# Entry to a paged decode stage: the order of the first key transposes, the third weight's cast, a zero fill and a third store buffer

## The chip, the cores and the metric

The kernel runs on one core of a Trainium2 chip. The metric is the device time of one execution in microseconds (us), lower is better. A core has TensorE (PE in the profile, with its weight loads as PEld), VectorE (DVE), ScalarE (ACT), GpSimd (POOL) and SyncE (SP). SP, ACT and POOL also issue DMA transfers, all of which run on the same 16 DMA engines of the core. Each engine works through its own instructions in their order; an instruction that waits for another engine or for a transfer holds up all that stands behind it on its engine.

## What is computed

The reference is one layer of a hybrid decoder for 512 prompt tokens and 32 sample tokens (8 sequences of 4), model width 1024:

```
h = x + 0.5 * post1(SwiGLU_1(pre1(x)))
u = pre_mix(h); z = u @ w_in
    4 HGRN2 heads: gated linear recurrence
    4 MLA heads: softmax attention on 256 latent + 64 rotary columns
h = h + post_mix(concat(o_hgrn, o_mla) @ w_out)
y = h + 0.5 * post2(SwiGLU_2(pre2(h)))
```

The sample tokens attend to 4096 past positions, which lie in a paged pool in HBM and are gathered through a page table. All is float32. The kernel forms a float32 product of two matrices as three products of float32r parts: each operand is split into a high part (a cast) and a low part (the operand less its high part), and high x high, high x low and low x high are added up in PSUM.

## The kernel before

Activations lie transposed, 128 features on the partitions and tokens along the free dimension. A weight is loaded in blocks of 128 output columns: `weight` (L211 to L220) issues a 512 KB load on SP's queue into one of five buffers `wraw`, casts it on ACT to the high part (L218) and subtracts on DVE for the low part (L219). The parts go to one of two buffer pairs `wh`, `wl`, or to a buffer that the caller passes as `home`. A raw buffer is free again after the subtract, and only then can SP load the next weight into it.

The stages follow each other: the first SwiGLU block (up to 390 us in the profile), the input projection with the recurrent heads (to 600), prompt attention (to 700), a long stage in which the decode attention of the sample tokens runs beside the output projection of the second prompt half and the first third of the second SwiGLU block (700 to 980), and the rest of the second SwiGLU block.

The change lies in the entry to that long stage, and in one buffer near its end. Two generators share the engines there. `phase_a` (L719) is the dense side. It starts with `project(1, ...)` (L664): the output projection of prompt half 1 in eight columns `d` of 128 features. Columns 0 and 1 are one `gemm_2` (L248), which does seven of the eight inner blocks of both and leaves the last, which needs the last attention head, to the end. Columns 2 to 7 are a `gemm_q` each (L237): 24 matmuls of 256 tokens. The weight `wo(d)` of columns 2 and 5 goes to a home of its own, a tile with the tag `hl`, so that it does not wait for `wh` and `wl`; the others rotate through the two pairs. In before, the cast and the subtract of `wo(2)` are written behind the two columns of `gemm_2` and their copies out of PSUM (`column`, L682). Beside this runs `squares(0)` (L706), which stores the finished half 0 and sums its squares (L711, L713). After the projection come SwiGLU columns of 512 prompt tokens (`gate`, `up`), and after every four of them `downs` (L751): eight partial products `d`, each copied out of PSUM by ACT (L755) into a tile `sit`, of which there are two, and stored to HBM from ACT's queue (L756). `downs` runs twice; the second pass (c = 1) lies at 944 to 978 us. Beside its last columns runs `sample_u` (L1345), whose sum of squares (L1364 on ACT, then the product at L1331 on PE) stands in the same queues.

`decode` (L1532) is the other side. For each half sequence (`Half`) it gathers two blocks of latent rows of 1 MB each (`gather`, L1455, POOL's queue) and two blocks of rotary rows of 256 KB (`gather_r`, L1464), then transposes them in five turns on DVE (`turn`, L1471, ten transposes of 32x32 blocks called `kh`), multiplies them with the queries (`score`, L1479), and so on. The first turn of a half takes the rotary blocks `rraw`, the other four the latent blocks (`ma` and `dx` for the first half). The weights of the softmax are spread into a tile `pbuf` (L1443), whose other places must be zero: POOL fills it (L1444), in before as the first thing in the stage, ahead of the gathers.

The two generators are advanced in turns by a fixed rule (L1616 to L1627); a scheduling pass then sets each engine's order. `tc.issue_after(i)` puts the instructions of its block behind instruction `i` in the order of their engine. `turn` uses it already for a half's last turn.

Of the kernel before, what the change touches and what calls it, by code (L numbers as in the profile page):

```python
# [8 lines left out]
F32 = mybir.dt.float32  # L9
# [5 lines left out]
ALU = mybir.AluOpType  # L15
# [92 lines left out]
def hybrid_step_kernel(  # L108
# [18 lines left out]
    def mk(shape, dt, tag, bufs=1, pool=None):  # L127
        return (pool or cur[-1]).tile(shape, dt, name=tag, tag=tag, bufs=bufs)
# [16 lines left out]
    def f32(ap):  # L145
        return ap.bitcast(F32)
# [61 lines left out]
    def rstd_u(u, x):  # L208
        return rstd(u[2], sumsq([h[x][:, k] for k in range(KD)]), D)

    def weight(srcs, kt, staged=False, home=None):  # L211
        pool, sfx, bufs = (st, "x", STAG) if staged else (sb, "", NW)
        w = mk([P, 8, P], F32, "wraw", 5, pool=sb)
        wh, wl = home or [mk([P, 8, P], F32R, n + sfx, bufs, pool=pool) for n in ("wh", "wl")]
        n = P // len(srcs)
        for i, s in enumerate(srcs):
            nc.sync.dma_start(w[:, :kt, i * n : (i + 1) * n], s)
        nc.scalar.copy(wh[:, :kt], w[:, :kt])  # L218
        nc.vector.tensor_tensor(wl[:, :kt], w[:, :kt], f32(wh[:, :kt]), op=ALU.subtract)  # L219
        return wh, wl, kt  # L220

    def mm3(out, pairs):
# [38 lines left out]
    def wcols(w, k0, kt, c0):  # L261
        return w[c0 // P, :, k0 : k0 + kt]
# [401 lines left out]
    def project(x, o, nxt, pool=None):  # L664
        if x:
            h[x] = actslot("m", 1, n=HS[0])
        else:
            qts.append(mk([P, 2 * KQ * HS[0]], F32, "q0", pool=dK))
            h[x] = qts[0][:, : KD * HS[0]].rearrange("p (k t) -> p k t", k=KD)
        nc.sync.dma_start(h[x], hsp[:, :, prompt[x]])  # L670
        yield
        mT = mk([P, KD, HS[0]], F32, "hh", pool=pool) if pool else actslot("m", x, n=HS[0])
        sacc = tmp("ssq", HS[0])

        def wo(d):
            home = None
            if pool and d % 3 == 2:
                home = mk([P, 2, KD, P], F32R, "hl", pool=pool)
                home = home[:, 0], home[:, 1]
            return weight([wcols(w_o, 0, KD, d * P)], KD, home=home)  # L680

        def column(d, acc):  # L682
            nc.scalar.copy(mT[:, d], acc)
            scale_sq(sacc, mT, d, gv, 3)

        d0 = 0
        if pool:
            for d, acc in enumerate((yield from gemm_2([wo(d) for d in range(2)], o))):
                column(d, acc)
            d0 = 2  # L690
            yield
        for d in range(d0, KD):
            column(d, (yield from gemm_q(wo(d), o, 4)) if pool else gemm(wo(d), o))
            yield
        yield from post(x, mT, sacc, None, nxt)

# [22 lines left out]
    def phase_a():  # L719
        acc = None  # L720
        full = slice(0, TP)

        def pair():
            return [mk([P, CA, TP], F32R, n, pool=ffa) for n in ("hh", "hl")]

        def col(w, f, cs=full, step=2):
            return gemm_q(w, [t[:, :, cs] for t in u4[:2]], step)

        def wt(w, f):
            return weight([wcols(w[1], 0, KD, f * P)], KD)  # L730

        def swish(s, z, cs):
            t = mk([P, TP], F32, "sit", 2, pool=ffa)[:, cs]
            nc.vector.tensor_tensor(s, z, u4[2][:, cs], op=ALU.mult)
            sigmoid(t, s)
            nc.vector.tensor_tensor(s, s, t, op=ALU.mult)

        def gate(f):
            s = mk([P, TP], F32, "sil", 1, pool=ffa)
            z = yield from col(wt(w_g, f), f)  # L740
            yield
            swish(s, z, full)
            return s

        def up(f, s):
            z = yield from col(wt(w_u, f), f)
            yield
            nc.vector.tensor_tensor(s, s, z, op=ALU.mult)
            split(hh[:, f % CA], hl[:, f % CA], s)

        def downs(c):  # L751
            for d in range(KD):
                acc = yield from gemm_q(weight([wcols(w_d[1], c * CA, CA, d * P)], CA), (hh, hl), 2)
                t = mk([P, TP], F32, "sit", 2, pool=ffa)
                nc.scalar.copy(t, acc)  # L755
                nc.scalar.dma_start(mA[c][:, d], t)  # L756
                yield

        pj = project(1, oo[1], to_ffn, ffa)
        next(pj)  # L760
        sq = squares(0)
        for n, _ in enumerate(pj):
            acc = next(sq, None) or acc
            if n == 9:
                root(0, acc)
            yield
            if n == 14:
                break
        s = mk([P, TP], F32, "sil", 1, pool=ffa)
        w, v = wt(w_g, 0), wt(w_u, 0)  # L770
        ups = []
        for x in BOTH:
            z = yield from col(w, 0, prompt[x], 4)
            yield
            ups.append((yield from col(v, 0, prompt[x], 4)))
            if x:
                root(1, acc)
            yield
            swish(s[:, prompt[x]], z, prompt[x])
            if x == 0:  # L780
                nc.vector.tensor_tensor(s[:, prompt[0]], s[:, prompt[0]], ups[0], op=ALU.mult)
                for _ in pj:
                    pass
                *_, acc = squares(1)
        hh, hl = pair()
        nc.vector.tensor_tensor(s[:, prompt[1]], s[:, prompt[1]], ups[1], op=ALU.mult)
        split(hh[:, 0], hl[:, 0], s)
        for c in range(FA // CA):
            for f in range(c * CA, (c + 1) * CA):
                if f:  # L790
                    s = ahead if f and f % CA == 0 else (yield from gate(f))
                    if f and f % CA == 0:
                        hh, hl = pair()
                    yield from up(f, s)
            if c + 1 < FA // CA:
                ahead = yield from gate(f + 1)
            yield from downs(c)
# [599 lines left out]
    with scope("dec"):  # L1397
# [43 lines left out]

        slots = ("ma", "dx0", "dx1", "q0", "ha", "hb", "mb")
        pbuf = mk([P, 2, 2, ROWS, 32], F32, "pbuf")  # L1443
        nc.gpsimd.memset(pbuf, 0.0)  # L1444
        NH2 = 2 * NB

        class Half:
# [84 lines left out]
        def decode():  # L1532
# [9 lines left out]
            def turn(top):  # L1542
                if ups:
                    h_, st = ups.pop(0)
                    with tc.issue_after(top.ins) if top is not None else nullcontext():
                        h_.turn(st)
                    if st == 0 and h_.n + 1 < NH2:
                        H[h_.n + 1].gather_r()

            for n in range(NH2 + 4):  # L1550
# [4 lines left out]
                for st in range(len(JS)):  # L1555
# [3 lines left out]
                    if n < 2 and st == 0:  # L1559
                        if n == 0:  # L1560
                            H[0].gather_r()
                        gather(2)
                    if n == 2 and st == 3:
                        gather(3)
                    if st == PEAK and at(3):
# [353 lines left out]
```

## Time and profile before

| what | value |
|---|---|
| time, median of 3 runs | 1246.13 us |
| the three runs | 1246.13, 1246.31, 1241.62 us |
| the profiled execution's own time | 1246.37 us |
| its span in the trace | 1244.6 us |
| PE busy | 1210.0 us, 97% of the span |
| DVE / ACT / POOL busy | 981.5 / 702.8 / 93.1 us |
| moved by DMA | 190.70 MB, 153 GB/s in the mean |

The profiled execution is 0.24 us above the median. Its time is 1.77 us longer than the span of its trace, which begins with the first and ends with the last instruction. In an answer of the trace, a row of the timeline gives the start, the duration, the engine, the line, the operation with its output and inputs, their shapes and how many such instructions were merged; in brackets stands the idle time of the engine just before, and what ended it. Matmuls overlap, so the distance of their starts, not their duration, is the pace. A row of the windows gives, for a stretch, each engine's busy time with the instructions in brackets, the granted TensorE clock (1.00 is full speed), the share of the DMA engines' time that was in use and the rate.

### The profile page before, as it was taken

How to read it: one execution, taken by the hardware profiler on the slowest of the kernel's cores; microseconds unless marked ns; L12 is line 12 of the kernel's file. 1: busy time of each engine (PE TensorE's matmuls, PEld its weight loads, DVE VectorE, ACT ScalarE, POOL GpSimd, SP SyncE). 2: the span in 40 equal slices, each digit the busy share in tenths (PEclk: the TensorE clock that was granted, in tenths of full speed). 3: DMA queues.
4: the chain of work that ended last, by engine and by line, in shares of the span. 5: the costliest groups of instructions: out<-in, count | busy, mean ns of one | idle time of the engine just before them, and what ended most of it. 6: DMA issues, size and time to landing. Idle time of an engine off the chain costs nothing.

```text
span 1244.6 us, 29432 instructions
## 1 busy us (share of the span) xinstructions
PE 1210.0 (97%) x12216; PEld 1114.2 (90%) x12216; DVE 981.5 (79%) x1994; ACT 702.8 (56%) x1524; POOL 93.1 (7%) x106
## 2 busy tenths in 40 slices
PE   8999999999999999999999799999999999999997
PEld 7999999999999989988998687776777899999996
DVE  7897788878678888786877779998885679778765
ACT  7675545444466745445758566555554446555373
POOL 0000000000000000000000212332320011000100
PEclk9999999999999999999999799999999999999998
DMA  6232333233164213333242676679775666833561
GB/s 238 86 119 87 101 103 102 86 102 98 52 228 141 79 59 100 100 82 102 93 137 82 216 276 204 227 277 358 267 258 169 242 242 231 226 120 103 117 146 73
DMA packets 80518, 190.70 MB, mean 153 GB/s; under 512 B 14064, under 2 KB 37648, under 8 KB 75904
## 3 DMA queue, kind: packets, MB, share of 16 engines
q1 hardware_dynamic: 58128, 115.50, 28.4%
q0 software_dynamic: 16368, 65.67, 16.2%
q10 hardware_dynamic: 5888, 7.65, 1.8%
q8 instruction: 96, 1.57, 0.5%
q14 instruction: 38, 0.31, 0.1%
HBM read 172.63 MB, written 16.16 MB: 152 GB/s over the span
## 4 chain that ended last, share of the span: by engine, by line
PE 80%; DVE 7%; issue 6%; DMA 4%; ACT 3%; POOL 0%; DVEq 0%; SPq 0%; POOLq 0%
PE acc L245 19%; PE dn L227 12%; PE Y L446 9%; PE acc L227 9%; PE Z L446 6%; PE X L446 6%; PE acc L1821 3%; PE acc L624 3%; PE s L1488 3%; PE o L1521 2%; DMA ma<-w_g 1%; DVE kh L1476 1%; PE pa L962 1%; PE s L1215 1%; DMA wraw<-w_u 1%
## 5 line engine op out<-in xcount | busy, mean ns | idle before, releaser
L245 PE MATMUL acc<-uh,wh 128*128 128x272 f32 (+2 forms) x496 | 161.7, 326 | 0.5 <-ACT uh L195 0.5
L245 PE MATMUL acc<-ul,wh 128*128 128x272 f32 (+2 forms) x496 | 156.6, 316 | 0.9 <-DVE ul L196 0.9
L245 PE MATMUL acc<-uh,wl 128*128 128x272 f32 (+2 forms) x496 | 155.7, 314 | 0.0
L219 DVE TENSOR_TENSOR wl<-wraw,wh 128x1024 fp32r<-128x1024 f32 (+2 forms) x78 | 83.8, 1075 | 37.0 <-ACT wh L218 36.7
L218 ACT CAST wh<-wraw 128x1024 fp32r<-128x1024 f32 (+2 forms) x78 | 72.6, 933 | 69.9 <-PE acc L245 62.4
L227 PE MATMUL dn<-hh,dh 128*128 128x272 f32 x384 | 111.6, 291 | 0.2 <-DVE hb L495 0.2
L227 PE MATMUL dn<-hh,dl 128*128 128x272 f32 x384 | 110.6, 288 | 0.0
L227 PE MATMUL dn<-hl,dh 128*128 128x272 f32 x384 | 110.5, 288 | 0.0
L245 PEld LDWEIGHTS acc<-uh,wh 128*128 128x128 f32 x496 | 93.3, 188 | 15.1 <-issue 9.9
L245 PEld LDWEIGHTS acc<-ul,wh 128*128 128x128 f32 x496 | 93.4, 188 | 7.1 <-issue 1.6
L245 PEld LDWEIGHTS acc<-uh,wl 128*128 128x128 f32 x496 | 93.3, 188 | 6.1 <-issue 1.1
L227 PEld LDWEIGHTS dn<-hh,dh 128*128 128x128 f32 x384 | 72.3, 188 | 1.4 <-DVE hb L495 0.4
L227 PEld LDWEIGHTS dn<-hl,dh 128*128 128x128 f32 x384 | 72.5, 189 | 0.0
L227 PEld LDWEIGHTS dn<-hh,dl 128*128 128x128 f32 x384 | 72.1, 188 | 0.0
L158 ACT CAST wh<-wraw 128x512 fp32r<-128x512 f32 (+1 forms) x67 | 41.0, 651 | 40.3 <-PE Z L446 22.6
L158 ACT CAST sh<-wraw 128x512 fp32r<-128x512 f32 (+1 forms) x66 | 40.6, 657 | 38.4 <-PE Z L446 26.0
L158 ACT CAST dh<-wraw 128x512 fp32r<-128x512 f32 x48 | 29.8, 621 | 45.5 <-PE dn L227 44.2
L159 DVE TENSOR_TENSOR wl<-wraw,wh 128x512 fp32r<-128x512 f32 (+1 forms) x67 | 47.1, 727 | 7.9 <-ACT wh L158 7.4
L1488 PE MATMUL s<-kh,q 64*32 64x128 f32 x2560 | 49.5, 273 | 2.3 <-issue 2.3
L1512 ACT COPY pbuf<-pt 32x64 f32<-32x64 f32 x192 | 46.5, 242 | 8.0 <-DVE pt L1508 5.2
L1488 PEld LDWEIGHTS s<-kh,q 64*32 64x32 f32 x2560 | 37.8, 105 | 13.7 <-issue 9.8
L159 DVE TENSOR_TENSOR sl<-wraw,sh 128x512 fp32r<-128x512 f32 (+1 forms) x66 | 46.7, 736 | 1.9 <-ACT sh L158 0.8
(720 smaller groups left out, 4117.2 us busy)
## 6 DMA issues: line engine op xcount, KB each, us to landing
wraw<-w_u SPq DMA_DIRECT2D x44, 512.0 KB, 4.0
wraw<-w_g SPq DMA_DIRECT2D x43, 512.0 KB, 3.7
wraw<-w_d SPq DMA_DIRECT2D x24, 512.0 KB, 3.9
wraw<-w_in SPq DMA_DIRECT2D x24, 512.0 KB, 3.6
wraw<-w_o SPq DMA_DIRECT2D x16, 512.0 KB, 3.6
wraw<-w_d SPq DMA_DIRECT2D x16, 384.0 KB, 3.1
wraw<-w_d SPq DMA_DIRECT2D x16, 256.0 KB, 4.1
mA<-sit ACTq DMA_DIRECT2D x16, 256.0 KB, 5.5
```

The costliest lines, as they stand in the source:

```text
L158: nc.scalar.copy(hi, src)
L159: (eng or nc.vector).tensor_tensor(lo, src, f32(hi), op=ALU.subtract)
L218: nc.scalar.copy(wh[:, :kt], w[:, :kt])
L219: nc.vector.tensor_tensor(wl[:, :kt], w[:, :kt], f32(wh[:, :kt]), op=ALU.subtract)
L227: nc.tensor.matmul(out, a, b, start=n == 0, stop=n == last)
L245: nc.tensor.matmul(acc[:, :n], a[:, k], b[:, k], start=k + i == 0, stop=k == kt - 1 and i == 2)
L446: nc.tensor.matmul(bank, a[p][:, k], b[q][:, k], start=first and k + n == 0, stop=k == 3 and n == 2, skip_group_check=True)
L624: nc.tensor.matmul(accs[x, d], wts[d][p][:, k], hs[k // 2][q][:, k % 2, x], start=k + n == 0, stop=k == nf - 1 and n == 2)
L1488: nc.tensor.matmul(self.s[r][c * 32 : c * 32 + 32, :P], q[rs, j], kh, start=st + jj == 0, stop=st == len(JS) - 1 and jj == 1, skip_group_c ...
L1512: (nc.scalar.copy if g else nc.vector.tensor_copy)(self.p[g * 32 : g * 32 + 32, c // 2, c % 2 * 4 : c % 2 * 4 + 4, self.i * 16 : self.i * ...
L1521: nc.tensor.matmul(o[g : g + 32, :R], self.p[:, c, a], self.craw[c][:, a], start=i + c == 0 and a < 4, stop=i + c == 2 and a >= 4, skip_gr ...
L1821: nc.tensor.matmul(accs[x, d], wts[d][p][:, k], hs[k // 2][q][:, k % 2, x], start=k + n == 0, stop=k == nf - 1 and n == 2)
```

## The change

Four edits:

1. `project` makes the weights of columns 0, 1 and 2 before the first product when it runs in `phase_a`. The cast and subtract of `wo(2)` so stand ahead of the copies of columns 0 and 1.
2. `weight` notes its subtract in `low`, `project` keeps that of `wo(3)` in `pin`, and the first turn of the first half goes through `issue_after` behind it.
3. The zero fill of `pbuf` is issued behind the first three gathers of latent rows.
4. In the second pass of `downs`, columns 2 and 5 use the tile `sil`, by then idle, as a third store buffer.

```diff
+    low = [None]
+    pin = [None]
...
-        nc.vector.tensor_tensor(wl[:, :kt], w[:, :kt], f32(wh[:, :kt]), op=ALU.subtract)
+        low[0] = nc.vector.tensor_tensor(wl[:, :kt], w[:, :kt], f32(wh[:, :kt]), op=ALU.subtract)
...
-            return weight([wcols(w_o, 0, KD, d * P)], KD, home=home)
+            w = weight([wcols(w_o, 0, KD, d * P)], KD, home=home)
+            if d == 3:
+                pin[0] = low[0]
+            return w
...
         if pool:
-            for d, acc in enumerate((yield from gemm_2([wo(d) for d in range(2)], o))):
+            w = [wo(d) for d in range(3)]
+            for d, acc in enumerate((yield from gemm_2(w[:2], o))):
                 column(d, acc)
             d0 = 2
             yield
         for d in range(d0, KD):
-            column(d, (yield from gemm_q(wo(d), o, 4)) if pool else gemm(wo(d), o))
+            wt = w[2] if pool and d == 2 else wo(d)
+            column(d, (yield from gemm_q(wt, o, 4)) if pool else gemm(wt, o))
...
-                t = mk([P, TP], F32, "sit", 2, pool=ffa)
+                n = c and d % 3 == 2
+                t = mk([P, TP], F32, "sil" if n else "sit", 1 if n else 2, pool=ffa)
...
         pbuf = mk([P, 2, 2, ROWS, 32], F32, "pbuf")
-        nc.gpsimd.memset(pbuf, 0.0)
...
                 if ups:
                     h_, st = ups.pop(0)
+                    if h_.n + st == 0:
+                        top = pin[0]
                     with tc.issue_after(top.ins) if top is not None else nullcontext():
                         h_.turn(st)
...
                         gather(2)
+                        if n:
+                            nc.gpsimd.memset(pbuf, 0.0)
```

Line numbers of the new kernel are up to twelve higher. On DVE at the entry to the stage, from the last step of half 0's activations (`ul`) on, this stood in before (`q_8242` is half 0 of the activations, `hl` is the weight of column 2, then of column 5, `wl` those of the columns between, `kh<-rraw` the two halves of the first key turn, `ssq` sums of squares):

```order
L196 SCALAR_TENSOR_TENSOR ul<-q_8242,gv,uh 128x256 x4
L268 TENSOR_TENSOR ssq<-ssq,sq_8856 128x256
L1476 STREAM_TRANSPOSE kh<-rraw 128x512
L713 TENSOR_TENSOR ssq<-ssq,sq_8860 128x256
L1476 STREAM_TRANSPOSE kh<-rraw 128x512
L219 TENSOR_TENSOR hl<-wraw,hl 128x1024
L713 TENSOR_TENSOR ssq<-ssq,sq_8881 128x256
L219 TENSOR_TENSOR wl<-wraw,wh 128x1024 x2
L1476 STREAM_TRANSPOSE kh<-ma 128x512 x3
```

And this stands there now:

```order
L196 SCALAR_TENSOR_TENSOR ul<-q_8242,gv,uh 128x256 x4
L222 TENSOR_TENSOR hl<-wraw,hl 128x1024
L271 TENSOR_TENSOR ssq<-ssq,sq_8860 128x256
L721 TENSOR_TENSOR ssq<-ssq,sq_8864 128x256
L721 TENSOR_TENSOR ssq<-ssq,sq_8880 128x256
L222 TENSOR_TENSOR wl<-wraw,wh 128x1024 x2
L222 TENSOR_TENSOR hl<-wraw,hl 128x1024
L271 TENSOR_TENSOR ssq<-ssq,sq_8896 128x256
L721 TENSOR_TENSOR ssq<-ssq,sq_8900 128x256
L1484 STREAM_TRANSPOSE kh<-rraw 128x512
L721 TENSOR_TENSOR ssq<-ssq,sq_8922 128x256
L1484 STREAM_TRANSPOSE kh<-rraw 128x512
```

The subtract for column 2 has moved to the front, and both transposes of the first key turn now stand behind the subtracts for columns 3, 4 and 5; those of the latent blocks follow between the subtracts for columns 6 and 7. On ACT, the last three columns of the second `downs` pass, from the cast of column 5's weight on, stood so in before (`mA` is the HBM buffer of the stores; the rows of L1355, L185, L186 and L1364 are those of `sample_u`):

```order
L218 CAST wh<-wraw 128x512
L755 COPY sit<-acc 128x512
L1355 ACTIVATE s_post<-tp 128x256
L756 DMA mA_4783<-sit 128x512
L158 CAST wh<-wraw 128x1024
L755 COPY sit<-acc 128x512
L185 ACTIVATE rs_t<-tS,epst 128x32
L756 DMA mA_4783<-sit 128x512
L186 ACTIVATE sS<-rs_t 128x32
L158 CAST wh<-wraw 128x1024
L755 COPY sit<-acc 128x512
L1364 ACTIVATE s_post<-ssq 128x256
```

And so now:

```order
L221 CAST wh<-wraw 128x512
L764 COPY sil<-acc 128x512
L1364 ACTIVATE s_post<-tp 128x256
L765 DMA mA_4783<-sil 128x512
L158 CAST wh<-wraw 128x1024
L764 COPY sit<-acc 128x512
L185 ACTIVATE rs_t<-tS,epst 128x32
L765 DMA mA_4783<-sit 128x512
L186 ACTIVATE sS<-rs_t 128x32
L158 CAST wh<-wraw 128x1024
L764 COPY sit<-acc 128x512
L1373 ACTIVATE s_post<-ssq 128x256
```

The order is the same, but column 5's copy has a buffer of its own, so that the copy of column 7 takes over the buffer of column 4's store and no longer that of column 5's.

## The prediction

> **What bounds the kernel now.** I read the page first, its slices of the span:
>
> ```profile
> PE   8999999999999999999999799999999999999997
> ```
>
> PE is over 90% busy in every slice except the first, the last and one in the middle, the 23rd (684 to 715 us). So PE paces the kernel, and time is to be had only where it waits. The view of the waits, for PE over the whole span, says where; its columns are total, number and longest:
>
> ```profile
> PE acc L245 <- DVE hl L219: 4.1, 1, 4.1
> PE acc L245 <- ACT hl L218: 3.3, 1, 3.3
> PE pr L1331 <- ACT s_post L1364: 2.6, 1, 2.6
> ```
>
> The first two are one place: column 2 of the projection waits for the high and then the low part of its weight `hl`. The third lies some 270 us later. Next I read the stretches around both places; behind the busy times stand clock, DMA share and GB/s:
>
> ```profile
> 702.00:704.00 2.00, 0.00 (x0) 0.00 (x0) 0.88 (x3) 2.00 (x7) 1.40 (x3) 0.59 1.00 334
> 701.66:709.80 8.14, 0.80 (x3) 0.50 (x2) 4.02 (x9) 5.44 (x12) 6.02 (x7) 0.54 0.97 317
> 709.80:715.95 6.15, 6.14 (x29) 6.15 (x30) 5.55 (x8) 1.05 (x2) 0.78 (x1) 0.50 1.01 420
> 715.95:730.20 14.25, 14.25 (x117) 14.09 (x117) 8.94 (x15) 11.03 (x25) 1.18 (x1) 1.00 0.81 302
> 978.13:982.20 4.07, 4.07 (x19) 4.02 (x20) 3.01 (x5) 1.34 (x4) 0.00 (x0) 0.59 0.43 165
> 982.20:984.45 2.25, 2.25 (x19) 2.21 (x18) 2.25 (x3) 0.00 (x0) 0.00 (x0) 0.99 0.00 0
> 984.45:1015.00 30.55, 30.32 (x376) 28.17 (x375) 21.27 (x28) 13.91 (x27) 4.21 (x6) 1.00 0.55 201
> ```
>
> Each stall costs twice. From 701.66 to 709.80 PE gets three matmuls in; then it runs 6.15 us at half clock, 29 matmuls at 0.212 us, where the next stretch needs 0.122 us each (14.25 / 117). At that pace the 29 take 3.53 us, so 2.62 us are lost to the clock. After the later stall 19 matmuls take 4.07 us, and the next 19 take 2.25. The first 19 hold two of another shape, so I don't take the whole 1.82 us; by the clock alone 4.07 x (1 - 0.59) = 1.67 is lost, and I use 1.7.
>
> Why is `hl` late? On DVE and ACT, ahead of the stall's end:
>
> ```profile
> 700.79 1.67 DVE L196 SCALAR_TENSOR_TENSOR ul<-q,gv,uh 128x256 fp32r<-128x256 f32 x4
> ...
> 707.00 0.71 DVE L1476 STREAM_TRANSPOSE kh<-rraw 128x512 f32<-128x512 f32 x1 [3.68 <-DMA rraw<-pool_r,idx]
> ...
> 708.57 1.18 DVE L219 TENSOR_TENSOR hl<-wraw,hl 128x1024 fp32r<-128x1024 f32 x1
> ```
>
> ```profile
> 700.00 1.71 ACT L195 ACTIVATE uh<-q,gv 128x256 fp32r<-128x256 f32 x4
> ...
> 703.86 1.04 ACT L218 CAST hl<-wraw 128x1024 fp32r<-128x1024 f32 x1
> ...
> 705.11 1.98 ACT L218 CAST wh<-wraw 128x1024 fp32r<-128x1024 f32 x2
> ```
>
> ```profile
> 709.80 0.80 PE L245 MATMUL acc<-ha,hl 128*128 128x256 f32 x2 [4.06 <-DVE hl L219]
> ```
>
> DVE stands 3.68 us before the first key transpose until the rotary rows land; the subtract for column 2 is queued behind it and starts at 708.57, and PE goes on 0.05 us after it ends. ACT's cast came at 703.86, behind the copies of columns 0 and 1.
>
> **The change, part by part.**
>
> *Third weight first, key turn behind the fourth.* In the new order ACT casts `hl` right behind `uh`, which ends at 701.71: 1.04 us later it is 702.75. DVE's `ul` ends at 702.46, so its subtract runs from 702.75 to 703.95 (1.18, rounded up), and with the 0.05 PE goes on at 704.00 instead of 709.80: **5.80 us**. That PE was then out of work since 701.66 still costs it 2.3 us. What is late next? Column 3 needs its two parts at 704.00 + 22 x 0.212 = 708.7 (half clock) or 706.7 (full). ACT loses no time over the reordering, the cast has only moved ahead of the copies: the casts `wh` of columns 3 and 4 stay at 705.11 to 707.09, with subtracts of some 1.2 us each to 707.4 and 708.6. So nothing at half clock, some 0.3 us at full clock, as four high products stand ahead of the first low one there. The copies of columns 0 and 1 come 1.04 us later, and only the fifth column needs their banks.
>
> Which stalls could the moved key turn make? The transposes of the first two turns (`rraw`, then `ma` and `dx`) now stand between the subtracts of columns 5 and 7, and wait for the same landings:
>
> ```profile
> dx<-pool_c,idx POOLq DMA_INDIRECT x1, 8.4
> ```
>
> ```profile
> wraw<-w_o SPq DMA_DIRECT2D x1, 512.0 KB, 7.7
> ```
>
> ```profile
> 699.76 0.95 POOL L1444 MEMSET pbuf<- 128x1024 f32 x1 [57.38 <-PE o L1247]
> 700.89 1.47 POOL L1468 DMA_INDIRECT rraw<-pool_r,idx  x1 [0.18 <-DVE hb L159]
> ...
> 705.21 0.94 POOL L1461 DMA_INDIRECT dx<-pool_c,idx  x1 [0.31 <-issue]
> ```
>
> `dx`, the last of these, landed at 705.21 + 8.4 = 713.6. Column 7 starts at about 720.8 (704.00, 24 matmuls a column at these paces), and its low part needs 0.7 (transpose) + 0.8 (two sums) + 1.2 (subtract) behind the landing: in time up to 718. The rest of SP's loads for the columns is asked for when a raw buffer comes free, so 5.8 us earlier too: the one of column 7 at 704.0 instead of 709.8, into a burst at 0.97 to 1.01 of the DMA engines. Taking its 7.7 us and half as much again for the busier queue, it lands by 715.6, and is wanted by 718. I price both at 0; the cover is 2 to 4 us, and what exceeds it is lost.
>
> *The clock.* Two idle gaps ahead of column 2 remain, and the matmul after which PE runs dry at 701.66,
>
> ```profile
> 700.16 0.50 PE L256 MATMUL acc<-ha,wh 128*128 128x256 f32 x2 [0.46 <-ACT ha L158]
> 700.93 0.39 PE L256 MATMUL acc<-hb,wh 128*128 128x256 f32 x1 [0.27 <-DVE hb L159]
> ...
> 701.39 0.28 PE L256 MATMUL acc<-ha,wl 128*128 128x256 f32 x1
> ```
>
> and the new gaps are 1.0 and 0.8 us. In 702 to 704 the mean clock is 0.59, which is full clock for 0.36 us and half clock after: it fell at 702.4, when PE had been out of work for 0.7 us. I therefore expect it to fall again. How long it stays low: 6.15 us after the first resumption, about 4.1 after the second; bounds for now are 0 and 6.15, I take their mean where it fell, 5.1. That loses 5.1 x (1 - 0.122 / 0.212) = 2.17 instead of 2.62: **0.45 us**. The Trainium skill ("TensorE: Matmul & The Clock Gate", Part 1: The HAM clock gate) has it that the clock falls after at least one idle window of about 3.4 us. By that rule the new gaps would leave it at full speed; the row above, with the fall 0.7 us after the last matmul, speaks against it.
>
> *Zero fill.* It freed POOL 1.13 us late (699.76 to 700.89), so the gathers start 1.1 us earlier. No PE wait hangs on that now: 0, at most 1.1 gained. In its new place it lies ahead of the next rotary gathers, which wait for the first key turn to free their buffers anyway, and `pbuf` is first written behind the first scores.
>
> *Third store buffer.* ACT near the end of the second pass, then PE, then the issue of column 4's store and its time to landing:
>
> ```profile
> 968.52 0.33 ACTq L756 DMA_DIRECT2D mA<-sit  x1
> ...
> 973.61 1.05 ACT L158 CAST wh<-wraw 128x1024 fp32r<-128x1024 f32 x1 [1.05 <-PE acc L245]
> 977.18 0.59 ACT L755 COPY sit<-acc 128x512 f32<-128x512 f32 x1 [2.52 <-DMA mA<-sit]
> 977.66 0.42 ACT L1364 ACTIVATE s_post<-ssq 128x256 f32<-128x256 f32 x1
> ```
>
> ```profile
> 978.13 0.48 PE L1331 MATMUL pr<-s_post,ones 128*128 128x256 f32 x1 [2.56 <-ACT s_post L1364]
> ```
>
> ```profile
> L756 ACTq DMA_DIRECT2D mA<-sit x1: 326/326/326, 963.6 to 963.6; - x1
> DMA to landing us min/median/max: 3.0/3.0/3.0
> ```
>
> Column 7's copy stood until the store of column 5, issued at 968.52, had landed 8.7 us later. Now it takes column 4's buffer, issued at 963.6 and landed at 966.6. It can start when the cast ends (974.66), 2.52 us earlier; `s_post` is done at about 975.55, and PE asks for it at 975.57. So PE's 2.56 us go, and with them the slow clock: **2.56 + 1.7 = 4.26 us**. Bounds: 0, if another store is late, and 4.4.
>
> *Sum.* 5.80 + 0.45 + 2.56 + 1.7 = 10.5 us, against the profiled execution's 1246.37: 1235.9. That execution lies 0.24 above the median 1246.13, so no correction. The gain should reach the end: the slices behind the entry are all at 9 but the last, from 984.45 to 1015 PE idles for 0.23 of 30.55 us, and loads and gathers start when PE, ACT or DVE free a buffer, so they move with them.
>
> **Rivals.**
>
> *The clock stays up at the entry.* Then 2.62 instead of 0.45 is gained, less 0.3 for column 3: 1246.37 - 12.4 = 1234.0. For it: the new gaps are 1.0 and 0.8 us, against 8 before; this is the page's rule. Against: the fall at 702.4. Chance 0.20.
>
> *The wait moves.* Transposes or loads in the denser burst exceed their cover by 2 to 6 us; 1238 to 1242. For it: the DMA share of 0.97 to 1.01; a gather that took 8.4 us to land. Against: the cover of 2 to 4 us. Chance 0.12, half of it above 1240.
>
> *The store buffer does nothing.* Another store is as late as that of column 5; then 4.26 are not gained, 1240.2. Against: column 4's store has 8 us to spare. Chance 0.10.
>
> *Slower.* The loads asked for earlier push the gathers of the first key turns back, DVE stands before them with the subtracts of columns 6 and 7 behind, and PE with it. Each us of `dx` past 718 costs one; past 728.5 all 10.5 are gone, and the time passes 1246. At the 420 GB/s of the burst that is over 6 MB more ahead of `dx`, while the early loads are three of 0.5 MB. Chance 0.03.
>
> That the first turn doesn't move can be excluded: the order shows it behind column 5's subtract.
>
> **How the numbers follow.** The forecast, 1235.9, gets 0.55. A measurement of this kernel can tell about 0.5% from no change, which is 6.2 us, or 1239.9. Faster: 0.55 + 0.20 + 0.06 (half of the moved wait) = 0.81. The same: 0.06 + 0.10 = 0.16. Slower: 0.03. The range goes from 1232.5, the clock case with the 1.1 us of the zero fill and rounding, to 1241.0, which takes in the store rival and most of the moved wait; some 0.1 is left out.
>
> **What would show it.** Right: PE's waits on `hl` at the entry fall from 7.3 to about 1.8 us in all, the first at 702.7, the second to 704.0; `kh<-rraw` comes without a wait; the gate columns of the next block start at 723 to 724 instead of 730.2; the wait of L1331 is gone and the clock is 1.00 there. Wrong: PE waiting in columns 5 to 7 for `wl` behind `kh<-ma` or `kh<-dx`; a copy `sit` or `sil` that waits for `mA`; a clock of 1.00 all through the entry; or new PE idle time behind 724 that gives the gain back.

## The result, and the profile after

| | before | changed |
|---|---|---|
| median | 1246.13 us | 1237.03 us |
| lowest and highest of five runs | 1241.62, 1246.31 | 1235.34, 1239.54 |
| the profiled execution's own time | 1246.37 | 1235.82 |
| its span in the trace | 1244.6 | 1234.0 |
| PE busy | 1210.0 | 1207.3 |

The ratio is 0.9928, with a 95% interval of 0.9912 to 0.9945: faster by 9.1 us in the medians and by 10.55 us between the two profiled executions. I forecast 1235.9 in a range of 1232.5 to 1241.0.

PE's slices of the span, in the page of the changed kernel; the 7 in the middle is gone:

```profile
PE   8999999999999999999999899999999999999997
```

The waits of PE over the whole span (total, number, longest), the lines that concern this change. Those on `hl` fell from 7.4 to 1.8 us, the one on `s_post` is gone, and one of 0.4 on a weight block is new:

```profile
PE acc L248 <- ACT hl L221: 1.0, 1, 1.0
PE acc L248 <- DVE hl L222: 0.8, 1, 0.8
PE sr L1326 <- DMA ma<-w_u: 0.4, 1, 0.4
```

The entry on PE, from the last head's first product to the first gate product:

```profile
700.50 0.50 PE L259 MATMUL acc<-ha,wh 128*128 128x256 f32 x2 [0.46 <-ACT ha L158]
701.27 0.39 PE L259 MATMUL acc<-hb,wh 128*128 128x256 f32 x1 [0.28 <-DVE hb L159]
...
703.03 0.39 PE L248 MATMUL acc<-ha,hl 128*128 128x256 f32 x1 [1.02 <-ACT hl L221]
...
704.30 0.80 PE L248 MATMUL acc<-ha,hl 128*128 128x256 f32 x2 [0.76 <-DVE hl L222]
...
724.61 0.28 PE L248 MATMUL acc<-uh,wh 128*128 128x256 f32 x1
```

DVE and POOL at the same place. The key transposes have no bracket, so DVE did not stand before them. The rotary gathers (`rraw`), at 700.89 in before, now run at 674.99, 26 us earlier:

```profile
712.56 0.70 DVE L1484 STREAM_TRANSPOSE kh<-rraw 128x512 f32<-128x512 f32 x1
...
717.27 0.70 DVE L1484 STREAM_TRANSPOSE kh<-dx 128x512 f32<-128x512 f32 x1
```

```profile
674.99 1.31 POOL L1476 DMA_INDIRECT rraw<-pool_r,idx  x1 [32.22 <-PE s L1226]
676.60 0.99 POOL L1476 DMA_INDIRECT rraw<-pool_r,idx  x1 [0.30 <-issue]
701.65 1.19 POOL L1469 DMA_INDIRECT ma<-pool_c,idx  x1 [24.05 <-ACT uh L195]
```

The clock at the entry in three windows (length, PE with its matmuls, and so on; the third number from the right is the clock). It is 1.00 up to 703.56, then half speed for two windows, 6.8 us, where it was half for 13.7 us in before:

```profile
700.15:703.56 3.41, 1.75 (x8) 1.13 (x8) 3.20 (x8) 3.41 (x9) 1.61 (x2) 1.00 0.46 140
703.56:706.97 3.41, 2.67 (x12) 2.68 (x13) 2.35 (x5) 3.41 (x8) 3.10 (x3) 0.50 0.98 298
706.97:710.39 3.42, 3.42 (x18) 3.42 (x17) 1.92 (x2) 1.46 (x3) 0.52 (x1) 0.50 1.01 386
```

ACT at the end of the second down pass. Column 5 is stored from `sil`, and column 7's copy starts at 967.90 without a wait:

```profile
961.86 0.33 ACTq L765 DMA_DIRECT2D mA<-sil  x1
964.68 0.58 ACT L764 COPY sit<-acc 128x512 f32<-128x512 f32 x1
...
967.90 0.58 ACT L764 COPY sit<-acc 128x512 f32<-128x512 f32 x1
968.38 0.42 ACT L1373 ACTIVATE s_post<-ssq 128x256 f32<-128x256 f32 x1
```

PE takes `s_post` at 968.86. With these rows and those of before the 10.6 us of span can be laid out by stages. Up to the last head's first product the changed run is 0.34 us later (700.50 against 700.16). From there to the first gate product it needs 24.11 us instead of 30.04: 5.93 gained. From the gate product to the issue of column 5's store it needs 237.25 instead of 238.32: 1.07. From there to the product with `s_post` 7.00 instead of 9.61: 2.61. From there to the end 265.14 instead of 266.47: 1.33. I put that down to the clock behind the old stall, less the new wait of 0.4 us; no run takes it apart. The sum is 10.60.

### The profile page after: what moved, and what is told of

Its sections match the earlier page's. It is cut to its first block, busy times and chain, and to the rows that moved or that the text cites. A ratio compares the mean times of both kernels' runs of the same rounds, so it can differ in the third digit from the quotient of the medians.

```text
span 1234.0 us, 29432 instructions
## 1 busy us (share of the span) xinstructions
PE 1207.3 (98%) x12216; PEld 1112.1 (90%) x12216; DVE 980.4 (79%) x1994; ACT 702.6 (57%) x1524; POOL 94.8 (8%) x106
## 4 chain that ended last, share of the span: by engine, by line
PE 81%; DVE 7%; issue 5%; ACT 4%; DMA 3%; POOL 0%; DVEq 0%; SPq 0%; POOLq 0%
PE acc L248 18%; PE dn L230 12%; PE acc L230 10%; PE Y L449 10%; PE X L449 7%; PE Z L449 6%; PE acc L1833 3%; PE acc L627 3%; PE s L1496 3%; PE o L1529 2%; DVE kh L1484 1%; DMA ma<-w_g 1%; PE pa L971 1%; PE s L1224 1%; DMA wraw<-w_u 1%
```

## The experiments

The runs were made on four chips; which chip the first two profiles come from is not on record. On three of the four the kernel before took 1257.9 to 1259.4 us, on the last 1246.65, so each run is set beside the kernel before on its own chip. The kernel before has a trace from the first profile only. "Entry" is the time in the trace from the last head's first product to the first gate product; "half clock" is the time at half clock between 700 and 732.

| run | edits | us | before, same chip | ratio and interval | entry | half clock |
|---|---|---|---|---|---|---|
| before (first profile) | none | 1246.13 | | | 30.04 | 13.7 |
| changed (first profile) | 1, 2, 3, 4 | 1237.03 | 1246.13 | 0.9928 (0.9912 to 0.9945) | 24.11 | 6.8 |
| e1_store | 4 | 1255.14 | 1257.85 | 0.9978 (0.9966 to 0.9990) | 29.44 | 10.2 |
| e2_entry | 1, 2 | 1252.19 | 1257.85 | 0.9956 (0.9943 to 0.9969) | 24.17 | 3.4 |
| e3_pin | 2 | 1258.73 | 1257.85 | 1.0004 (0.9991 to 1.0017) | 30.61 | 10.2 |
| e4_early | 1 | 1255.77 | 1257.85 | 0.9989 (0.9979 to 0.9999) | 27.80 | 6.8 |
| e9_fill | 3 | 1256.85 | 1259.41 | 0.9982 (0.9971 to 0.9994) | 27.39 | 6.8 |
| e7_fillback | 1, 2, 4 | 1250.11 | 1258.69 | 0.9932 (0.9912 to 0.9951) | 24.74 | 3.4 |
| e10_nopin | 1, 3, 4 | 1251.15 | 1259.41 | 0.9938 (0.9926 to 0.9951) | 24.47 | 6.8 |
| e13_nocast | 2, 3, 4 | 1239.82 | 1246.65 | 0.9940 (0.9919 to 0.9960) | 27.26 | 6.8 |
| e8_sil2 | 1, 2, 3, 4 for column 2 only | 1252.92 | 1258.69 | 0.9948 (0.9931 to 0.9965) | 24.17 | 6.8 |
| e11_after | 1, 2, 3, 4 | 1249.02 | 1259.41 | 0.9915 (0.9900 to 0.9929) | 22.98 | 3.4 |
| e5_ahead | all, and one step more | 1243.96 | 1258.69 | 0.9888 (0.9861 to 0.9915) | 19.87 | 0 |
| e12_ahead_again | the same | 1244.33 | 1259.41 | 0.9883 (0.9867 to 0.9900) | 19.87 | 0 |

My theory: the entry and the late store are two separate stalls, each with its own stretch of half clock; edits 1 and 2 end the first, edit 4 the second, edit 3 does nothing. The rivals: one of the edits does all at the entry; the store falls right once the entry is shorter; the fill has a part.

### The store buffer: e1_store and e8_sil2

e1_store is the kernel before with edit 4 alone:

```diff
-                t = mk([P, TP], F32, "sit", 2, pool=ffa)
+                n = c and d % 3 == 2
+                t = mk([P, TP], F32, "sil" if n else "sit", 1 if n else 2, pool=ffa)
```

> The kernel before with the third store buffer alone. Theory (two separate stalls, each with its own slow clock): the wait of the sum of squares at the end of the second down pass goes with the clock loss behind it, 2.56 + 1.7 = 4.3 us, so about 1241.9 us; the entry stays as it was, with waits of 3.3 and 4.1 us on the weight of column 2. Rival A (the late store comes from how the stores fall against the loads, and the buffer alone does not cure it): 1246. Rival B (the stall would have moved to the next place that waits on a store): 1244 to 1246, with a new wait on a store behind it.

The wait on `s_post` is gone there, column 7's copy follows its cast at once, and no new wait on a store appears at PE. The time is 2.7 us lower, with an interval of 1.3 to 4.3 that only just takes in the 4.26 I expected. The runs on these chips that keep two buffers or leave column 5 out wait 1.4 to 2.2 us for `s_post` (e3_pin 1.4, e4_early 1.9, e2_entry, e8_sil2 and e9_fill 2.2). One 3.4 us stretch of half clock costs 3.41 x (1 - 0.122 / 0.212) = 1.45 us. But it does not always come: behind that wait the clock fell in before, e2_entry, e4_early and e8_sil2, and stayed at 1.00 in e3_pin and e9_fill. This is e9_fill, over all of that place (the third number from the right is the clock):

```profile
980.00:1000.00 20.00, 17.81 (x171) 16.34 (x171) 14.46 (x19) 9.45 (x18) 1.41 (x2) 1.00 0.66 239
```

So by these numbers the edit is worth 1.4 to 3.7 us in one execution on these chips, and the 2.7 in the medians fits.

e8_sil2 is the changed kernel with the third buffer for column 2 but not for column 5:

```diff
-                n = c and d % 3 == 2
+                n = c and d == 2
```

> The changed kernel, but only column 2 of the second down pass uses the third store buffer, column 5 does not. Theory (column 7 waits for the store of column 5, because two buffers rotate; a third buffer helps only where it takes the late store out of the rotation): the wait of the sum of squares is back with about 2.6 us and half clock behind it, about 4.3 us slower than the changed kernel. Rival (the stores fall differently since the entry is shorter, or any third buffer gives slack): the changed kernel's time.

ACT and PE of e8_sil2:

```profile
985.51 0.59 ACT L764 COPY sit<-acc 128x512 f32<-128x512 f32 x1 [2.16 <-DMA mA<-sit]
985.99 0.42 ACT L1373 ACTIVATE s_post<-ssq 128x256 f32<-128x256 f32 x1
```

```profile
986.46 0.70 PE L1340 MATMUL pr<-s_post,ones 128*128 128x256 f32 x2 [2.20 <-ACT s_post L1373]
```

The wait is back, as long as in the other runs on these chips that keep it, with a third buffer in use and the entry as short as in the changed kernel. So neither slack nor the shift cures it: column 7 waits for the store of column 5, and of the two placements of a third buffer only the one that takes that store out of the rotation ends it. The theory holds.

### One edit at the entry alone: e3_pin, e4_early, e9_fill

e3_pin holds the first key turn back and does nothing else:

```diff
+            if d == 3:
+                pin[0] = low[0]
...
+                    if h_.n + st == 0:
+                        top = pin[0]
```

> The kernel before with the second edit alone: the first key turn goes behind the fourth weight's subtract, while the cast of column 2's weight stays behind the copies of columns 0 and 1. Theory: the cast still ends at 704.9, the subtract follows at once and ends at about 706.1, where it ended at 709.75; so 3.7 us come from the pin alone, 1242.4 us, with waits of 3.3 us on the cast and about 0.8 on the subtract. Rival A (the turn was the whole cause): 1240.2. Rival B (without the early cast nothing is gained): 1246.

My number fell: nothing is gained. PE does go on 3.6 us earlier with column 2 (706.81, which is 6.04 us behind the last head's first product, 9.64 in before). But column 5's subtract stands behind transposes of latent rows, as it did in before. There DVE came to them so late that the rows had landed; now it comes earlier and waits for them. DVE, then PE, of e3_pin:

```profile
711.63 0.71 DVE L1482 STREAM_TRANSPOSE kh<-ma 128x512 f32<-128x512 f32 x1 [1.05 <-DMA ma<-pool_c,idx]
715.73 0.71 DVE L1482 STREAM_TRANSPOSE kh<-dx 128x512 f32<-128x512 f32 x1 [3.39 <-DMA dx<-pool_c,idx]
```

```profile
718.87 0.50 PE L248 MATMUL acc<-ha,hl 128*128 128x256 f32 x2 [0.96 <-DVE hl L222]
...
724.34 0.70 PE L179 MATMUL pr<-ssq,ones 128*128 128x256 f32 x2 [1.88 <-DVE ssq L719]
```

PE stands 0.96 us for column 5 and 1.88 for the sum of squares of half 0, which DVE adds up behind those transposes, and then runs another 3.4 us at half clock. The wait moved, and the gain was lost.

e4_early is the first edit alone:

```diff
-            for d, acc in enumerate((yield from gemm_2([wo(d) for d in range(2)], o))):
+            w = [wo(d) for d in range(3)]
+            for d, acc in enumerate((yield from gemm_2(w[:2], o))):
...
+            wt = w[2] if pool and d == 2 else wo(d)
```

> The kernel before with the first edit alone: column 2's weight is cast and subtracted ahead of everything, but the first key turn is not held back and now stands ahead of the subtracts of columns 3 and 4. Theory: PE goes on with column 2 near 704, as in the changed kernel, then waits up to 1 us for the low part of column 3, since the transposes wait for the rotary rows until 707 and the subtract of column 3 ends near 709.8, wanted at about 709; 4.8 to 5.4 us gained, 1241.0 us, so the two edits overlap and don't add up. Rival A (the pin is what counts, the cast alone only moves the wait one column on): 1244 to 1246. Rival B (the early cast is enough, the pin does nothing): 1240.2 and no wait in column 3.

Rival A came nearer: 2.1 us in the medians, 0.1 to 2.6 by the interval. PE resumes as early as in the changed kernel, but DVE then stands before the first key transpose until the rotary rows land; a square on ACT waits for a sum on DVE behind it, and on ACT the casts of columns 3 and 4 stand behind that square. DVE, ACT and PE of e4_early:

```profile
708.42 0.71 DVE L1478 STREAM_TRANSPOSE kh<-rraw 128x512 f32<-128x512 f32 x1 [3.75 <-DMA rraw<-pool_r,idx]
```

```profile
709.47 0.42 ACT L713 ACTIVATE sq<-q 128x256 f32<-128x256 f32 x1 [3.81 <-DVE ssq L268]
709.79 1.98 ACT L218 CAST wh<-wraw 128x1024 fp32r<-128x1024 f32 x2
```

```profile
710.88 0.58 PE L245 MATMUL acc<-ha,wh 128*128 128x256 f32 x1 [3.27 <-ACT wh L218]
```

I had expected 1 us in column 3, on its low part; it was 3.27 on its high part, by a way over two engines that I had not followed.

e9_fill is the third edit alone:

```diff
-        nc.gpsimd.memset(pbuf, 0.0)
...
                         gather(2)
+                        if n:
+                            nc.gpsimd.memset(pbuf, 0.0)
```

> The kernel before with the third edit alone, the later zero fill. In the kernels with the fill at the front, POOL stood 57.4 us before it until a product of the last attention head freed its place, and the rotary gathers were queued behind it, from 701; in the changed kernel they were issued at 675. Theory: the 3.7 us that DVE stood before the first key transpose come from the fill. With it gone the subtract of column 2 follows its cast at about 706.1 instead of 709.75, and PE gains 3.7 us there; but the transposes of the latent rows then stand ahead of column 5's subtract and wait for their landing, as with the pin alone, which gives part of it back: 0 to 3 us faster than before. Rival (my prediction's reading: the fill costs its own 1.1 us and no more): no change, DVE still waits over 2 us for the rotary rows.

As the theory of that run has it. POOL, DVE and PE of e9_fill:

```profile
675.35 1.31 POOL L1467 DMA_INDIRECT rraw<-pool_r,idx  x1 [32.26 <-PE s L1217]
```

```profile
703.08 0.71 DVE L1475 STREAM_TRANSPOSE kh<-rraw 128x512 f32<-128x512 f32 x1
```

```profile
706.92 0.80 PE L245 MATMUL acc<-ha,hl 128*128 128x256 f32 x2 [0.47 <-DVE hl L219]
...
722.57 0.70 PE L179 MATMUL pr<-ssq,ones 128*128 128x256 f32 x2 [1.92 <-DVE ssq L713]
```

With nothing changed but the fill's place, the 3.68 us that DVE stood before the first key transpose are gone. So that wait came from the fill. That it held up column 2's subtract came from the order: e3_pin, with the fill in front, frees column 2 just as early. 2.6 us are gained; 1.92 are lost again at the sum of squares, by the same order as in e3_pin.

### One edit left out: e2_entry, e7_fillback, e10_nopin, e13_nocast, beside e11_after

e2_entry is the kernel before with edits 1 and 2, whose lines stand above.

> The kernel before with the first two edits (third weight cast first, first key turn behind the fourth weight's subtract); the zero fill and the store buffers are as they were. Theory: the entry gives what it gave in the changed kernel, 5.6 to 6.0 us, and the wait of the sum of squares near 972 stays at about 2.6 us with half clock behind it: about 1240.2 us. Rival A (the earlier start already changes how the stores fall, so the late store goes without the third buffer): 1236. Rival B (the zero fill had a part in it, the key rows land too late without its move): 1241 to 1242, with waits in columns 5 to 7.

5.7 us, as the theory has it, and the wait on `s_post` stays (2.21 us). But there is a wait of 1.1 us on half 0's sum of squares, so rival B is not wrong either. e7_fillback shows it with the store buffer in place:

```diff
         pbuf = mk([P, 2, 2, ROWS, 32], F32, "pbuf")
+        nc.gpsimd.memset(pbuf, 0.0)
...
-                        if n:
-                            nc.gpsimd.memset(pbuf, 0.0)
```

> The changed kernel with the zero fill back at the front of the stage, ahead of the gathers. Theory: the fill delays the gathers by about 1.1 us, the key turn has more room than that, so PE sees nothing: the time of the changed kernel within 0.3 us. Rival (the fill's move was needed for the turns of the first half to keep ahead of columns 5 to 7): 1 us slower, with waits of PE on a weight's low part behind a key transpose.

DVE, then PE, of e7_fillback:

```profile
717.72 0.71 DVE L1485 STREAM_TRANSPOSE kh<-dx 128x512 f32<-128x512 f32 x1 [1.71 <-DMA dx<-pool_c,idx]
```

```profile
719.12 0.70 PE L179 MATMUL pr<-ssq,ones 128*128 128x256 f32 x2 [1.66 <-DVE ssq L721]
```

The rival is right, but for the place: with the fill at the front the gather of `dx` is issued at 705.5, lands at 717.7, and PE waits 1.66 us, for the sum of squares and not for a weight's low part. This run, e2_entry and e11_after have one stretch of half clock each at the entry. The entry of this run is longer than that of e11_after by 24.74 - 22.98 = 1.76, that of e2_entry by 24.17 - 22.98 = 1.19. The ratios of this run and e11_after differ the same way (0.9932, 0.9915), but their intervals overlap; the trace carries this, not the times.

e11_after is the changed kernel itself.

> The changed kernel itself, beside the kernels below and the kernel before on one chip. The chips of the earlier runs were some 11 us slower for the kernel before, with 6 to 8 us of PE's idle time in the scores that was 2 us in the first profiles. Theory: the gain does not depend on that, 8.5 to 10.5 us below the kernel before, with the same waits on column 2's weight (1.0 and 0.8 us). Rival (part of the gain was how the two first executions fell): 6 to 8 us.

10.4 us below the kernel before: the gain is there on this chip too, where both kernels take longer.

e10_nopin leaves edit 2 out:

```diff
-                    if h_.n + st == 0:
-                        top = pin[0]
```

> The changed kernel without the second edit: early cast, later zero fill and third buffer, but the first key turn is not held back; its first transpose stands ahead of column 2's subtract. Theory: since the rotary rows have landed long before, the transpose costs only its own 0.7 us; the subtract ends 0.5 us later than in the changed kernel and nothing else waits, 0.3 to 0.8 us slower than the changed kernel, so the pin has almost nothing left to do. Rival (the pin is what keeps DVE free): DVE waits for the rotary rows ahead of the subtracts of columns 2 to 4, and 3 to 6 us of the gain are gone.

PE's wait on the low part of column 2 is 1.04 us instead of 0.76, and nothing else waits; beside the changed kernel's run with the same 6.8 us of half clock the entry is 0.36 longer (24.47, 24.11). In the medians of one chip it is 2.1 us slower than e11_after; the profiled executions of the two differ by one stretch of half clock, some 1.45 us. So by the traces the pin is worth some 0.4 us once the fill is out of the way; that the rest of the 2.1 is the clock is argued from one execution of each.

e13_nocast leaves edit 1 out:

```diff
-            w = [wo(d) for d in range(3)]
-            for d, acc in enumerate((yield from gemm_2(w[:2], o))):
+            for d, acc in enumerate((yield from gemm_2([wo(d) for d in range(2)], o))):
```

> The changed kernel without the first edit: the key turn is held back and the fill is late, but column 2's weight is cast behind the copies of columns 0 and 1 again. In this order three transposes of latent rows stand ahead of column 5's subtract. Theory: PE waits 3.3 us for the cast and 0.5 us for the subtract, 2 us more than in the changed kernel, and then up to 2 us for the sum of squares queued behind the transposes that wait for the latent rows, so from the last head's first product to the first gate product it takes 26.5 to 28 us, where the changed kernel took 23.0 and 24.1: 2.5 to 4 us slower than the changed kernel, 6 to 8 us below the kernel before. Rival (pin and fill are enough, the cast's place is worth only its own 2 us or nothing): within 2 us of the changed kernel.

The entry takes 27.26 us, in the expected range, with waits of 3.27 and 0.46 on column 2 and 1.68 on the sum of squares; 6.8 us are gained over before. PE of e13_nocast:

```profile
705.51 0.58 PE L248 MATMUL acc<-ha,hl 128*128 128x256 f32 x1 [3.27 <-ACT hl L221]
...
722.41 0.70 PE L179 MATMUL pr<-ssq,ones 128*128 128x256 f32 x2 [1.68 <-DVE ssq L719]
```

With the same 6.8 us of half clock the changed kernel's entry is 3.15 us shorter (24.11). So of the three edits at the entry the cast can least be spared, the fill is worth 1.2 to 1.8, and the pin little.

### One step further: e5_ahead and e12_ahead_again

Here half 0's last four activation parts (`uh`, `ul`), wanted only by the gate columns, come behind column 2's weight; the weights of columns 3 and 4 are made right behind the first two columns, and the pin is column 5's subtract:

```diff
-PJ = (0, 0, 0, 0, 4, 4, 2, 1)
+PJ = (0, 0, 0, 0, 4, 4, 2, 0)
...
-            if d == 3:
+            if d == 5:
                 pin[0] = low[0]
...
-            for d, acc in enumerate((yield from gemm_2(w[:2], o))):
+            accs = yield from gemm_2(w[:2], o)
+            w += [wo(3), wo(4)]
+            for d, acc in enumerate(accs):
...
-            wt = w[2] if pool and d == 2 else wo(d)
+            wt = w[d] if pool and d < 5 else wo(d)
...
         for n, _ in enumerate(pj):
+            for _ in pj0 if n == 0 else ():
+                pass
...
+    pj0 = pj
     gb = phase_a()
+    next(gb)
...
-        ib = 0
+        ib = 1
```

> The changed kernel, with column 2's weight cast and subtracted one step earlier still: ahead of the last four parts of half 0's activations, which nobody needs before the gate columns; the weights of columns 3 and 4 are made right behind the first two columns, and the first key turn is held behind column 5's subtract. The low part should be there at about 702.7, so that PE waits 0 on the cast and about 0.6 us on the subtract, where it waits 1.0 and 0.8 in the changed kernel: 1.5 us gained by the waits. For the clock there are two theories. A: it falls whenever the few us around are idle enough, as in both kernels so far, and the gaps left (0.5, 0.3, 0.6 us) are too short to do it: another 2.4 us, in all 3.9 below the changed kernel, about 1233. B: it falls at any gap here: 1.5 us below, about 1235.5, with half clock for 3 to 7 us. Against both: the activations that come later are wanted by the gate columns, or the key turn's later place makes columns 6 and 7 wait: no gain.

> The version with column 2's weight made ahead of the last parts of half 0's activations, once more and now beside the changed kernel on one chip. Theory: no fall of the clock at the entry, waits of 0.5 us in all on column 2's weight, 3 to 5 us below the changed kernel. Rival: it gained by how that chip's executions fell, and is within 2 us of the changed kernel here.

PE of e12_ahead_again, and the stretch behind the first of these rows:

```profile
702.77 0.51 PE L248 MATMUL acc<-ha,hl 128*128 128x256 f32 x2 [0.46 <-DVE hl L222]
...
721.61 0.39 PE L248 MATMUL acc<-uh,wh 128*128 128x256 f32 x1 [0.78 <-ACT wh L221]
```

```profile
704.00:710.00 6.00, 6.00 (x52) 6.00 (x52) 5.00 (x8) 6.00 (x16) 2.91 (x3) 1.00 0.96 335
```

One wait of 0.46 us is left on column 2, the clock stays at 1.00, and PE does 52 matmuls in a stretch in which the changed kernel did 26 (5.70 us at clock 0.50). The entry takes 19.87 us in both runs. A new wait of 0.78 us, on the cast of a gate weight, follows 1.2 us behind the entry's end in both and is not in that figure. On one chip this version takes 1244.33 where the changed kernel takes 1249.02, and the intervals only touch (0.9867 to 0.9900, 0.9900 to 0.9929): the lowest ratios of all. That is in the 3 to 5 us that e12 expected. The traces explain part of it: of the 5.2 us between the two profiled spans (1248.3, 1243.1) 3.11 lie in the entry, and 1.73 ahead of it, which this edit does not account for. Clock theory A fits the entry. But in e12_ahead_again the clock fell twice for one window each later in the stage, at 770.7 and 832.1, and in e5_ahead, the same kernel, not at all up to 1230 us.

## Why the prediction was right, and where it was not

**PE goes on at 704.00 instead of 709.80, 5.80 us.** Right: 704.30 in a run that was 0.34 us later already, so 5.84. The first gate product came at 724.61, just past the 723 to 724 that I had named.

**The clock at the entry, 0.45 us.** Here the step failed that took a mean, "bounds for now are 0 and 6.15, I take their mean where it fell, 5.1". The half clock lasted until 710.39, 6.1 us behind the point where PE went on; that costs 6.1 x (1 - 0.122 / 0.212) = 2.6 us, as much as before, so the term was nothing. In e11_after, with the same gaps of 1.0 and 0.8 us, it was one stretch of 3.4 us. In e4_early the same two gaps (1.03, 0.78) brought no fall; the clock fell there only in the next wait, of 3.27 us. The term is no size of the kernel; it goes in steps of 1.45 us from one execution to another.

**The moved key turn, "I price both at 0; the cover is 2 to 4 us".** Right for the whole change, for a reason that I did not give. I took 8.4 us for the landing of `dx`; in the changed kernel its two gathers took 12.0 and 13.6:

```profile
DMA to landing us min/median/max: 12.0/12.8/13.6
```

The first was issued 2.1 us earlier than in before, at 703.14, and so was there at 715.1; DVE asked for it at 717.27. Without the fill's move the cover is short, by 1.1 us of PE's time in e2_entry and 1.7 in e7_fillback. And the first to be late is not the low part of column 7, as I had it, but the product with half 0's sum of squares (L179), whose additions on DVE stand behind `kh<-dx`. My "wait moves" rival was the very thing that happens in e2, e3, e7, e9 and e13, with waits of 1.1 to 2.8 us.

**The zero fill, "It freed POOL 1.13 us late (699.76 to 700.89), so the gathers start 1.1 us earlier".** This step is wrong. I read the fill's own 0.95 us from its row and passed over the bracket at its end, 57.38 us of standing until a product of the last head released its place. The rotary gathers were queued behind that wait; they now start 26 us earlier, and the latent ones 2.3 us earlier (701.65, 703.96). This was the cause of the 3.68 us that DVE stood for the rotary rows (e9_fill); I had taken that wait as given and only moved the transposes out of its way.

**The third store buffer, 2.56 + 1.7 us.** Right: 2.61 to the product, and 1.33 + 0.39 = 1.72 behind it. e8_sil2 shows that it hangs on column 5. The second number is in part luck: in e3_pin and e9_fill the same wait, 1.4 and 2.2 us long, brought no half clock, so there was not always something to gain.

**The sum.** Three things went against the sum: some 0.4 too much for the clock, 0.34 for a run that was later ahead of the entry, and the new 0.39 us for `ma<-w_u`. Together 1.1, they were made up by 1.07 us that I had not forecast: between the gate product and column 5's store PE was idle and busy a little less at many places, which no run here takes apart. So the profiled 10.55 beside my 10.5 is partly luck, and it hides that the fill's move, which I put at nothing, was needed to keep all of the 5.80. The median gain, 9.1, is 1.4 us less: the profiled execution is the second lowest of five.

**The rivals.** The clock did not stay up: it fell at 703.56, 0.8 us before PE went on. That is what the earlier fall in before had let me expect. It was not certain, as e4_early shows with the same gaps; in e12_ahead_again, with gaps of 0.46, 0.27 and 0.46 us, it stayed up at the entry. That the store buffer does nothing is excluded by e1_store and e8_sil2, and nothing of the slower case appeared: `dx` was there before DVE asked for it.

## What to carry to other kernels

An instruction that costs 1 us but waits 57 us in a queue of its engine costs what is queued behind it: read the bracket of every row that a change moves, and list what stands behind, before its duration. Three edits at one stall are not three terms: take the stall's chain apart (cast, subtract, transposes, their landing, the gathers' queue) and ask of each edit alone what is late next. If a stall is short, count the idle time of some 3.4 us around it: about half a window of idle time was enough here for a clock step.

## What the runs showed of the hardware

The time at half clock between 700 and 732 us was 0, 3.4, 6.8, 10.2 or 13.7 us in all traces, whole multiples of 3.41 us. Here is e4_early in windows of that length, laid from where the clock changed: two windows at full speed, then the one after which it fell, one at half, and the one after which it rose.

```profile
699.59:703.00 3.41, 2.09 (x14) 1.55 (x13) 3.41 (x8) 2.51 (x6) 2.31 (x2) 1.00 0.16 46
703.00:706.42 3.42, 2.19 (x16) 1.99 (x17) 1.45 (x2) 2.66 (x8) 2.51 (x4) 1.00 1.01 300
706.42:709.83 3.41, 1.18 (x10) 0.98 (x9) 1.33 (x3) 0.36 (x2) 1.84 (x3) 0.97 1.02 352
709.83:713.24 3.41, 2.21 (x8) 1.92 (x9) 3.31 (x5) 3.41 (x7) 1.47 (x2) 0.50 1.00 418
713.24:716.65 3.41, 3.41 (x19) 3.41 (x18) 3.41 (x7) 1.19 (x4) 0.00 (x0) 0.53 1.01 426
```

And before, up to its fall at 702.36:

```profile
698.95:702.36 3.41, 1.98 (x13) 1.44 (x12) 3.41 (x8) 2.62 (x8) 2.42 (x2) 1.00 0.17 57
```

With such windows laid over the 13 traces in which the clock fell, from 10 to 1225 us, it fell behind every window in which PE was busy for 1.60 us or less and behind none with more than 2.28. In between it went both ways. In e9_fill it stayed up behind 1.61 us of work (720.77 to 724.18); in e12_ahead_again it fell behind 2.28 (828.69 to 832.10). So busy time as the profile has it sets no sharp threshold. It stayed low behind 2.79 us and less, and rose only behind a full window. The gaps of 1.0 and 0.8 us with those at the head's last products leave 1.6 to 1.8 us of work where one window holds most of them, and there the clock fell. In e4_early a border of two windows lay inside the first of the two; these windows held 2.09 and 2.19 us, the first two rows above, and it stayed up. So both whether the changed kernel falls and how long it pays depend on where the window lies. The Trainium skill ("TensorE: Matmul & The Clock Gate", Part 1: The HAM clock gate) gives a free-running window of 3413 ns; the multiples agree. Its condition for the fall, at least one idle window, does not: before fell behind a window with 1.98 us of work, and the changed kernel behind one with 1.75.

The kernel before took 1257.9 to 1259.4 us on three chips, 1246.65 on a fourth and 1246.13 in the first profiles. In the first of these two rows of waits, of the changed kernel in its first profile and in e11_after, PE stands before score products for 2.0 us in all, in the second for 7.6, and the profile shows nothing that it waits for; PE is also busy for 9.7 us more (1217.0, 1207.3). What makes this difference stays open.

```profile
PE s L1496 <- issue: 2.0, 2, 1.2
```

```profile
PE s L1496 <- issue: 7.6, 20, 1.4
```
